# Pooling's projections and four of six gate slabs as seven products of two by two blocks, ahead of HGRN2

## The chip, the cores and the metric

The kernel runs on one core of a Trainium2 chip. The metric is the device time of one launch in microseconds (us); lower is better. Before the change it is 1067.72 us, the median of three runs (1067.62 to 1069.56).

## What is computed

One layer of a hybrid sequence model, on 1024 tokens of 1024 channels, float32. The input is normed and multiplied by one wide matrix `w_in` of 6668 columns. Its columns feed three mixers and their gates. The mixers' results are gated, multiplied by `w_out`, added to the input, and a second gate (`w_pg`) and a last norm follow.

```
u = rms_norm(h, norm_w);  proj = u @ w_in
q, f_logit, i_in, g_hg, u_pool, g_pool, xbc, dt_raw, z = split(proj)
#  768 768   768   768   512     512    1792  12      768  columns
o_hg   = group_rms_norm(hgrn2(q, f_logit, i_in), hg_norm_w) * silu(g_hg)
o_pool = pool_mixer(u_pool) * silu(g_pool)      # windowed means, then a 128x128 matrix per group
y_ssd  = ssd_mixer(xbc, dt_raw) * silu(z)       # state space mixer, normed afterwards
h = h + concat(o_hg, o_pool, o_ssd) @ w_out
out = rms_norm(h + sigmoid(h @ w_pg) * (p @ w_pe))
```

## The kernel before, in words

Float32 products are made of three products of rounded parts (`mm3`, lines 166 to 169): each operand is split into `hi`, rounded, and `lo`, the rest. `u`, transposed, stands as `uh` and `ul` on chip for the whole first half. A weight is loaded into `raw` (two buffers, L135), cast to `hi` on ScalarE (L142) and subtracted to `lo` on VectorE (L143); there are four pairs of `hi` and `lo`. `wsplit` gives these two a priority of 400 steps, and evacuations of a result get 500.

There are two forms of projection. `cm_proj(j)` (L171) leaves 128 channels on the partitions and streams all 1024 tokens in two halves of 512: 48 matmuls of 128x512. `tm_tile` (L184) leaves 128 tokens on the partitions and streams 256 channels of a slab: 24 matmuls of 128x256 for each of eight token tiles.

The order of the program text is: the norm of x with the first slab of V; two more slabs of V (L271), evacuated into `O`, a part of the tile `big` (L233); small values of the state space mixer; six heads of HGRN2 (`hg_proj`, `hg_mix`), which read V from `O` and write their result there; the state space mixer, with 14 channel tiles (`conv_tile`) and four groups (`ssd_group`); three slabs of HGRN2's gate g (L618); pooling, with four times two channel tiles (L641 to 677); three slabs of the gate z (L710); the output projection in two halves of its rows (`ab`) and four slabs each (L742), whose operands overwrite `uh` and `ul` by `fill`; the last gate and norm. A planner places each instruction on its engine, taking ready work by priority (order in the text, moved up by the offsets above) and by estimated times; on the chip each engine then runs its own list in order. SyncE (SP) issues all the loads and stores spoken of here, in order too. Scratch space is handed out by an `Arena` over one tile of 13 x 1024 words, `ar`, the longest free first.

Of the kernel before, what the change touches and what calls it, by code (L numbers as in the profile page):

```python
# [46 lines left out]
class Arena:  # L47
    """Space of one tile, handed out in program order, the longest free first."""
# [29 lines left out]
def body(ctx: ExitStack, tc: tile.TileContext, x, pT, wcm, wtm, wdt, wo, wg, we, nw, fw, cst, prm, out):  # L78
# [9 lines left out]
    a2s = ctx.enter_context(ExitStack())  # L88
    a2p = a2s.enter_context(tc.tile_pool(name="a2p", bufs=1))
# [4 lines left out]
    a2w = 13 * 1024  # L94
    ar = Arena(a2p.tile([P, a2w], F32, name="ar"), a2w)
# [23 lines left out]
    acc = [big[:, 6144 + i * 1024 : 6144 + (i + 1) * 1024].rearrange("p (c t) -> p c t", t=P) for i in range(2)]  # L119
    blk = [cp.tile([P, NT, 32], F32, name=f"blk{i}") for i in range(2)]  # L120
    for a in blk + acc:
        G.memset(a, 0.0)
# [43 lines left out]
    def mm3(o, sh, sl, mh, ml, first, last):  # L166
        T.matmul(out=o, lhsT=sh, rhs=mh, start=first, stop=False)  # L167
        T.matmul(out=o, lhsT=sh, rhs=ml, start=False, stop=False)  # L168
        T.matmul(out=o, lhsT=sl, rhs=mh, start=False, stop=last)  # L169

    def cm_proj(j, evac):  # L171
        """channels of tile j by all tokens: evac(half, psum [P, 512])"""
        cm_want(j)
        hi, lo = pieces.pop(("c", j))
        for half in range(2):
            b = bank("pj")
            c = slice(half * 512, half * 512 + 512)
            for k in range(KD):
                w = slice(k * P, (k + 1) * P)
                mm3(b, hi[:, w], lo[:, w], uh[:, k, c], ul[:, k, c], k == 0, k == KD - 1)  # L180
            with tc.high_priority(offset=EPRIO):
                evac(half, b)
# [15 lines left out]
    def x_norm(t):  # L198
        xt, _ = xs_in[t]
# [4 lines left out]
    def x_turn(t):  # L204
        xt, h = xs_in[t]
        for q in range(2):
# [4 lines left out]
            split_out(b.rearrange("p (k t) -> p k t", t=P), slice(q * 4, q * 4 + 4), slice(t * P, (t + 1) * P))  # L211
        ar.give(h)

    def x_tile(t):
        x_norm(t)
        x_turn(t)

    def split_out(src, ks, cols, scale=None):
        """src -> uh (rounded) and ul (the rest)"""
        hi, lo = uh[:, ks, cols], ul[:, ks, cols]  # L220
        if scale is None:
            A.copy(hi, src)  # L222
            V.tensor_tensor(out=lo, in0=src, in1=hi.bitcast(F32), op=ALU.subtract)  # L223
# [4 lines left out]
    O = big[:, 0:6144].rearrange("p (c n) -> p c n", n=768)  # L228
    dtr = cp.tile([P, NT, NSH], F32, name="dtr")

    def v_evac(s):
        def f(t, b):
            A.copy(O[:, t, s * 256 : s * 256 + 256], b[:, :256])  # L233
# [8 lines left out]
    nc.sync.dma_start(xs_in[1][0], x[P : 2 * P, :])  # L242
    raws.append(wload(tm_src("v", 0)[0][1], 1024))
    for t in range(2, NT):
        nc.sync.dma_start(xs_in[t][0], x[t * P : (t + 1) * P, :])
    with tc.manual_schedule(engines={mybir.EngineType.DVE, mybir.EngineType.Activation, mybir.EngineType.Pool}):
# [22 lines left out]
    ar.give(nwb_h)  # L269
    ar.give(jx_h)  # L270
# [82 lines left out]
    def hg_mix(h):  # L353
# [9 lines left out]
        def scores(b, X, n, cs_):  # L363
            """b[s, c, :] = the keys of s by the queries X of its block of 32"""
# [6 lines left out]
        def place(b, w, nc_, c0, m0, lo, off, cnt, per):  # L371
            """masked columns [off, off + cnt) of each node of b -> columns lo.. of each node of w in the blocks"""
# [7 lines left out]
        def carry(w):  # L380
            """keys and decays from nodes of w to nodes of 2 w"""
# [8 lines left out]
        # within nodes of 4: the queries, decayed over 0, 1, 2 and 3 steps  # L390
# [10 lines left out]
        # queries decayed from their node's start: the first node of four into Q, the rest into XB  # L401
# [11 lines left out]
        # within nodes of 16  # L413
# [44 lines left out]
        # keys with tokens on partitions  # L458
# [10 lines left out]
        for c in range(NT):  # L469
# [37 lines left out]
    def conv_tile(j, nxt):  # L507
        """projection of channel tile j of xbc, convolution and silu: [P, S]"""
# [25 lines left out]
    xw = [big[:, 6144 + i * 768 : 6144 + (i + 1) * 768] for i in range(2)] + [cp.tile([P, 768], F32, name=f"xw{i}") for i in range(2)]  # L534
    nx = [0]

    def ssd_group(g, Bc, Cc):
# [12 lines left out]
        for c in range(NT):  # L550
            tk = slice(c * P, (c + 1) * P)
            r0 = c * NSH + 3 * g
            E = sp.tile([P, 3, P], F32, tag="E", bufs=3, name="E")
# [6 lines left out]
            cbm = sp.tile([P, P], F32, tag="cbm", bufs=2, name="cbm")  # L560
# [27 lines left out]
            if c < NT - 1:  # L588
                cur = sp.tile([P, DG], F32, tag="hst", bufs=2, name="hst")
# [8 lines left out]
    # tiles of xbc: x 0..5, B 6..9, C 10..13  # L598
    plan = ((0, (6, 10, 0, 1)), (1, (7, 11, 2)), (2, (8, 12, 3, 4)), (3, (9, 13, 5)))
    order = [12 + j for _, js in plan for j in js]  # L600
    for g, js in plan:
# [9 lines left out]
        if g == 3:  # L611
            tm_want("g", 0)
# [5 lines left out]
    for s in range(3):  # L618
        tm_want("g", s)
        pcs = [pieces.pop(("g", s, i)) for i in range(2)]  # L620

        def ge(t, b, s=s):
            sg = sp.tile([P, 256], F32, tag="sg", bufs=2, name="sg")
            A.activation(sg, b, AF.Silu)  # L624
            for i in range(2):
                h = 2 * s + i
                V.scalar_tensor_tensor(  # L627
                    out=O[:, t, h * P : (h + 1) * P], in0=O[:, t, h * P : (h + 1) * P], scalar=rsh[:, h, t : t + 1],
                    in1=sg[:, i * P : (i + 1) * P], op0=ALU.mult, op1=ALU.mult)

        for t in range(NT):
            tm_tile("g", s, 256, t, ge, pcs)
            if t == 4:
                if s < 2:
                    want(("g", s + 1, 0), tm_src("g", s + 1)[0][0], 1024)
                else:
                    cm_want(26)

# [1 line left out]
    PO = []  # L640
    for g, win in enumerate(WINS):  # L641
        (U, Uh), (B0, B0h), (B1, B1h) = ar.take(1024), ar.take(1024), ar.take(1024)

        def ue(half, b, U=U):
            A.copy(U[:, half * 512 : half * 512 + 512], b)

        cm_proj(26 + g, ue)
        cm_want(30 + g)
        src, bufs, d, n = U, [B0, B1], 1, 0
        while d < win:  # L650
            dst = bufs[n % 2]
            V.tensor_tensor(out=dst[:, d:], in0=src[:, d:], in1=src[:, : S - d], op=ALU.add)
            V.tensor_copy(dst[:, :d], src[:, :d])
            src, d, n = dst, 2 * d, n + 1
        dst = bufs[n % 2]
        V.tensor_tensor(out=src[:, : win - 1], in0=src[:, : win - 1], in1=cs[:, C_INV : C_INV + win - 1], op=ALU.mult)
        V.tensor_tensor(out=dst[:, : win - 1], in0=src[:, : win - 1], in1=U[:, : win - 1], op=ALU.subtract)
        V.scalar_tensor_tensor(out=dst[:, win - 1 :], in0=src[:, win - 1 :], scalar=1.0 / win, in1=U[:, win - 1 :], op0=ALU.mult, op1=ALU.subtract)
        ar.give(Uh)
        ar.give((B0h, B1h)[(n + 1) % 2])  # L660
        po, poh = ar.take(1024)
        PO.append((po, poh))

        def gpe(half, b, po=po):
            A.activation(po[:, half * 512 : half * 512 + 512], b, AF.Silu)

        cm_proj(30 + g, gpe)
        if g < 3:
            cm_want(26 + g + 1)
        else:  # L670
            tm_want("z", 0)
        for half in range(2):
            c = slice(half * 512, half * 512 + 512)
            b = bank("mx")
            T.matmul(out=b, lhsT=pr[:, P_PW + g * P : P_PW + (g + 1) * P], rhs=dst[:, c], start=True, stop=True)
            V.scalar_tensor_tensor(out=po[:, c], in0=b, scalar=pr[:, P_PS + g : P_PS + g + 1], in1=po[:, c], op0=ALU.mult, op1=ALU.mult)
        ar.give((B0h, B1h)[n % 2])

# [241 lines left out]
```

## Time and profile before

| | |
|---|---|
| median of the runs | 1067.72 us |
| the profiled execution, first to last instruction (its span) | 1066.3 us |
| TensorE matmul (PE) busy | 1044.2 us, 98% |
| VectorE (DVE) busy | 549.0 us, 51% |
| ScalarE (ACT) busy | 400.8 us, 38% |
| GpSimd (POOL) busy | 38.9 us, 4% |
| bytes moved by DMA | 63.83 MB |

No other time is given for the profiled execution than its span; the median of the runs is 1.4 us above it. Matmuls are pipelined: one lasts longer than the distance from it to the next, so the rate is read from start to start. A few per cent of the matmul records can be missing. In the rows, "idle <- X" is time in which an engine sat still, and what it was waiting for.

### The profile page before, as it was taken

The page shows a single profiled execution, that of the slowest core. Times are in us where ns is not written, and L with a number is a line of the kernel's source. Part 1 is how long each engine was busy: PE and PEld are TensorE (multiplying, and loading weights), DVE is VectorE, ACT ScalarE, POOL GpSimd, SP SyncE. Part 2 cuts the span into 40 slices and gives each one's busy share as a digit, 9 for nine tenths or more (in the row PEclk, how much of TensorE's full clock was granted, in tenths as well). Part 3 has the DMA queues.
Part 4 walks back from the last instruction along what each step waited for, and adds up shares of the span by engine and source line. Part 5 has one row for each costly group of instructions (what it writes and reads, how often), then busy time and mean ns, then how long its engine had stood idle before and what let it go on. Part 6 is the DMA issues. An engine that isn't in the chain of part 4 may idle for free.

```text
span 1066.3 us, 19848 instructions
## 1 busy us (share of the span) xinstructions
PE 1044.2 (98%) x8508; PEld 940.4 (88%) x8508; DVE 549.0 (51%) x1090; ACT 400.8 (38%) x842; POOL 38.9 (4%) x69
## 2 busy tenths in 40 slices
PE   8999999999999999999999999999999999999997
PEld 7998778777878788878999777999999999999997
DVE  6413766776674768577832224325532452354444
ACT  6424244323445566656722112126410330143323
POOL 2000000000001000000000000002100000000002
PEclk9999999999999999999999999999999999999999
DMA  7212101010101122122112111111223241111003
GB/s 289 82 41 84 41 21 41 22 41 21 41 21 41 65 75 79 41 79 61 38 44 76 40 40 40 40 41 41 70 87 127 66 139 40 41 41 41 2 19 140
DMA packets 23671, 63.83 MB, mean 60 GB/s; under 512 B 2624, under 2 KB 11168, under 8 KB 23328
## 3 DMA queue, kind: packets, MB, share of 16 engines
q1 hardware_dynamic: 23440, 62.52, 17.6%
q8 instruction: 66, 1.08, 0.4%
q14 instruction: 21, 0.17, 0.1%
q10 hardware_dynamic: 144, 0.07, 0.0%
HBM read 58.33 MB, written 4.24 MB: 59 GB/s over the span
## 4 chain that ended last, share of the span: by engine, by line
PE 85%; DVE 10%; ACT 2%; DMA 1%; POOL 1%; issue 1%; POOLq 0%; ACTq 0%; DVEq 0%
PE b_pj L167 24%; PE b_pj L168 24%; PE b_pj L169 24%; DVE ar L356 5%; PE b_mx L580 1%; PE b_sc L478 1%; PE b_mx L473 1%; PE b_mx L475 1%; DVE lo L143 1%; DVE blk L375 1%; PE b_sc L369 1%; DMA E<-cumd 1%; PE b_mx L688 1%; ACT hi L142 1%; PE b_mx L583 1%; PE b_mx L704 1%
## 5 line engine op out<-in xcount | busy, mean ns | idle before, releaser
L167 PE MATMUL b_pj<-hi,uh 128*128 128x256 f32 (+1 forms) x1344 | 380.2, 283 | 0.2 <-ACT uh L222 0.2
L168 PE MATMUL b_pj<-lo,uh 128*128 128x256 f32 (+1 forms) x1344 | 378.4, 282 | 0.2
L169 PE MATMUL b_pj<-hi,ul 128*128 128x256 f32 (+1 forms) x1344 | 378.1, 281 | 0.2 <-DVE ul L223 0.2
L167 PEld LDWEIGHTS b_pj<-hi,uh 128*128 128x128 f32 x1344 | 253.4, 189 | 1.0 <-ACT uh L222 0.5
L168 PEld LDWEIGHTS b_pj<-lo,uh 128*128 128x128 f32 x1344 | 252.9, 188 | 1.0 <-DVE lo L143 0.6
L169 PEld LDWEIGHTS b_pj<-hi,ul 128*128 128x128 f32 x1344 | 252.8, 188 | 0.5 <-DVE ul L223 0.4
L167 PE MATMUL b_pj<-uh,hi 128*128 128x512 f32 x544 | 220.0, 404 | 0.0
L169 PE MATMUL b_pj<-uh,lo 128*128 128x512 f32 x544 | 219.4, 403 | 0.0
L168 PE MATMUL b_pj<-ul,hi 128*128 128x512 f32 x544 | 218.5, 402 | 0.0
L143 DVE TENSOR_TENSOR lo<-raw,hi 128x1024 fp32r<-128x1024 f32 (+1 forms) x76 | 93.1, 1225 | 145.9 <-ACT hi L142 130.0
L142 ACT CAST hi<-raw 128x1024 fp32r<-128x1024 f32 (+1 forms) x76 | 79.7, 1048 | 206.1 <-PE b_pj L169 106.1
L168 PEld LDWEIGHTS b_pj<-ul,hi 128*128 128x128 f32 x544 | 102.3, 188 | 23.6 <-issue 0.7
L167 PEld LDWEIGHTS b_pj<-uh,hi 128*128 128x128 f32 x544 | 102.3, 188 | 23.2 <-ACT hi L142 0.7
L169 PEld LDWEIGHTS b_pj<-uh,lo 128*128 128x128 f32 x544 | 102.3, 188 | 22.9
L356 DVE TENSOR_TENSOR ar<-ar 128x512 f32<-128x512 f32 (+8 forms) x168 | 94.1, 597 | 6.5 <-PE b_sc L447 4.9
L522 DVE SCALAR_TENSOR_TENSOR ar<-ar,pr 128x1021 f32<-128x1021 f32 (+2 forms) x42 | 53.8, 1280 | 3.4 <-ACT ar L514 2.9
L556 ACT ACTIVATE E<-E,sm 128x128 f32<-128x128 f32 x96 | 32.3, 393 | 24.4 <-DMA E<-cumd 9.2
L766 DVE TENSOR_TENSOR big<-xr,b_pj 128x256 f32<-128x256 f32 x32 | 13.5, 420 | 48.9 <-PE b_pj L169 48.4
L768 DVE TENSOR_TENSOR big<-big,b_pj 128x256 f32<-128x256 f32 x32 | 13.4, 420 | 43.4 <-PE b_pj L169 43.4
L627 DVE SCALAR_TENSOR_TENSOR big<-big,rsh,sg 128x128 f32<-128x128 f32 x48 | 14.7, 349 | 28.8 <-ACT sg L624 28.7
L513 ACT COPY ar<-b_pj 128x512 f32<-128x512 f32 x28 | 16.3, 581 | 33.1 <-PE b_pj L169 33.1
L812 ACT ACTIVATE junk<-sg 128x256 f32<-128x256 f32 x32 | 13.4, 418 | 40.3 <-DVE sg L810 40.3
(184 smaller groups left out, 1066.6 us busy)
## 6 DMA issues: line engine op xcount, KB each, us to landing
raw<-wcm SPq DMA_DIRECT2D x34, 512.0 KB, 3.2
raw<-wtm SPq DMA_DIRECT2D x16, 512.0 KB, 3.3
raw<-wo SPq DMA_DIRECT2D x16, 512.0 KB, 3.4
E<-cumd SPq DMA_DIRECT2D x32, 192.0 KB, 3.0
ar<-x SPq DMA_DIRECT2D x8, 512.0 KB, 9.1
xr<-x SPq DMA_DIRECT2D x32, 128.0 KB, 2.4
raw<-wg SPq DMA_DIRECT2D x8, 512.0 KB, 3.5
out<-big SPq DMA_DIRECT2D x8, 512.0 KB, 2.6
```

The costliest lines, as they stand in the source:

```text
L142: A.copy(hi[:, :width], raw[:, :width])
L143: V.tensor_tensor(out=lo[:, :width], in0=raw[:, :width], in1=hi[:, :width].bitcast(F32), op=ALU.subtract)
L167: T.matmul(out=o, lhsT=sh, rhs=mh, start=first, stop=False)
L168: T.matmul(out=o, lhsT=sh, rhs=ml, start=False, stop=False)
L169: T.matmul(out=o, lhsT=sl, rhs=mh, start=False, stop=last)
L356: mul = lambda o, x, y: V.tensor_tensor(out=o, in0=x, in1=y, op=ALU.mult)
L513: A.copy(xp[:, c], b)
L522: V.scalar_tensor_tensor(out=y[:, d:], in0=xp[:, : S - d], scalar=cw(i), in1=y[:, d:], op0=ALU.mult, op1=ALU.add)
L556: A.activation(E[:, i, :], E[:, i, :], AF.Relu, scale=-1.0, bias=cum[:, r0 + i : r0 + i + 1])
L627: V.scalar_tensor_tensor(out=O[:, t, h * P : (h + 1) * P], in0=O[:, t, h * P : (h + 1) * P], scalar=rsh[:, h, t : t + 1], in1=sg[:, i * P ...
L766: V.tensor_tensor(out=H[:, t, qc], in0=xr, in1=b, op=ALU.add)
L768: V.tensor_tensor(out=H[:, t, qc], in0=H[:, t, qc], in1=b, op=ALU.add)
```

## The change

Strassen's scheme in Winograd's form: a product of two by two blocks in seven products of blocks instead of eight. `u` is cut into four blocks, two halves of the tokens by two halves of its 1024 channels; the weights into two halves of these channels by two tiles (or slabs) of columns. Each of the seven products runs through `mm3`, with half the depth (four steps of 128 instead of eight).

- `build_sums` makes four sums of blocks of `uh + ul` in `big` and splits them into eight tiles `SH`, `SL` of 128 x 2048, in a space of their own (`spool`). This stands after the slabs of V in the text, and may not be placed ahead of the last transposition of x.
- V no longer goes to `O`, since `big` is now the scheme's scratch space (an `Arena` called `bg`); it goes through a small tile to an array `vd` in DRAM and is loaded back into `O` ahead of HGRN2 (24 stores, 6 loads).
- Pooling stands ahead of HGRN2: `st_cm` computes two channel tiles at once, four times (84 matmuls of 128x512 instead of 96). Its gated result goes to `pod` in DRAM (four stores) and comes back at the output projection (four loads).
- `st_tm` computes two slabs at once, twice: z0 with z1, z2 with g0 (336 matmuls of 128x256 instead of 384). The silu of each goes to `gzd` in DRAM (32 stores of 128 KB). z comes back in eight loads in `z_gate`, called beside `y_norm` in the second slab of the output projection; g0 in eight loads beside the slab g1.
- g1 and g2 stay as they were, and the first `fill` moves from the slab z2 to the slab g2.
- `ar` and its pool are opened after the scheme's space is closed. The small tile `sg` has four buffers instead of two, and `xr` shares them.

```diff
+    sst = ctx.enter_context(ExitStack())
+    spool = sst.enter_context(tc.tile_pool(name="spool", bufs=1, reuse_waits="tile"))
+    SH = [spool.tile([P, 4, 512], F32R, name=f"sh{i}") for i in range(4)]
+    SL = [spool.tile([P, 4, 512], F32R, name=f"sl{i}") for i in range(4)]
...
+    def build_sums():
+        for i, j in ((1, 0), (1, 1), (0, 0), (0, 1)):
+            V.tensor_tensor(out=quad(uf, i, j), in0=quad(uh, i, j).bitcast(F32), in1=quad(ul, i, j).bitcast(F32), op=ALU.add)
+        V.tensor_tensor(out=Q22, in0=Q21, in1=Q22, op=ALU.add)
+        V.tensor_tensor(out=Q21, in0=Q11, in1=Q21, op=ALU.subtract)
+        V.tensor_tensor(out=Q11, in0=Q22, in1=Q11, op=ALU.subtract)
+        V.tensor_tensor(out=Q12, in0=Q12, in1=Q11, op=ALU.subtract)
+        for q, hi, lo in zip((Q22, Q11, Q21, Q12), SH, SL):
+            A.copy(hi, q)
+            V.tensor_tensor(out=lo, in0=q, in1=hi.bitcast(F32), op=ALU.subtract)
...
+    def st_cm_w(j0, j1):
+        r0, r1 = wload(wcm[j0], 1024), wload(wcm[j1], 1024)
...
+        w0 = wsplit(r0, 1024)
+        with tc.high_priority(offset=WPRIO):
+            V.tensor_tensor(out=t1, in0=b12, in1=b11, op=ALU.subtract)
+            V.tensor_tensor(out=t3, in0=b22, in1=b12, op=ALU.subtract)
+        w1 = wsplit(T_[:, :1024], 1024)
+        with tc.high_priority(offset=WPRIO):
+            V.tensor_tensor(out=t2, in0=t3, in1=b11, op=ALU.add)
+            V.tensor_tensor(out=t4, in0=b21, in1=t2, op=ALU.subtract)
+        w2 = wsplit(T_[:, 1024:], 1024)
+        w3 = wsplit(b22, 512)
...
+        return {1: part(w0, 0), 2: part(w0, 1), 5: part(w1, 0), 7: part(w1, 1), 6: part(w2, 0), 4: part(w2, 1), 3: part(w3, 0)}
...
+    def st_cm(W, o0, o1):
+        X, Y, Z = bank("mx"), bank("pj"), bank("sc")
...
+        prod(X, 1, True)
+        cp_(o0[:, h0], X)
+        prod(Y, 5, True)
+        cp_(o1[:, h1], Y)
+        prod(X, 6, False)
+        cp_(o1[:, h0], X)
+        prod(Z, 2, True)
+        add_(o0[:, h0], Z)
+        prod(X, 7, False)
+        add_(o1[:, h1], X)
+        prod(Y, 3, False)
+        add_(o1[:, h0], Y)
+        prod(X, 4, False)
+        cp_(o0[:, h1], X)
...
+    def st_tm(s0, s1, fin):
...
+        X = [bank("mx") for _ in range(4)]
+        w4()
+        for o, i in ((c11, 1), (c12, 6), (c22, 7)):
+            for t in prod(X, i, i == 1):
+                with tc.high_priority(offset=EPRIO):
+                    A.copy(o[t], X[t][:, :256])
+            {1: w5, 6: w3, 7: w2}[i]()
+        for t in prod(X, 4, False):
+            fin(4 + t, 0, X[t][:, :256])
+        Y = [bank(("pj", "sc")[t // 2]) for t in range(4)]
+        for o, i in ((c22, 5), (c12, 3)):
+            for t in prod(Y, i, i == 5):
+                with tc.high_priority(offset=EPRIO):
+                    V.tensor_tensor(out=o[t], in0=o[t], in1=Y[t][:, :256], op=ALU.add)
+                fin((4 if i == 5 else 0) + t, 1, o[t])
...
+    W = st_cm_w(26, 27)
+    for g0 in (0, 2):
+        (U0, U0h), (U1, U1h) = bg.take(1024), bg.take(1024)
+        st_cm(W, U0, U1)
+        W = st_cm_w(30 + g0, 31 + g0)
...
+        st_cm(W, G0, G1)
+        if g0 == 0:
+            W = st_cm_w(28, 29)
+        for (g, U, Uh), Gt in zip(pos, (G0, G1)):
+            A.activation(Gt, Gt, AF.Silu)
+            V.tensor_tensor(out=U, in0=U, in1=Gt, op=ALU.mult)
+            nc.sync.dma_start(pod[g], U)
...
+    for i, slabs in enumerate(((5, 6), (7, 2))):
+        def gz_fin(t, n, b, i=i):
+            sg = sp.tile([P, 256], F32, tag="sg", bufs=4, name="sg")
+            with tc.high_priority(offset=EPRIO):
+                A.activation(sg, b, AF.Silu)
+            nc.sync.dma_start(gzd[:, t, (2 * i + n) * 256 : (2 * i + n) * 256 + 256], sg)
...
+    sst.close()
...
+    for h in range(HEADS):
+        nc.sync.dma_start(O[:, :, h * P : (h + 1) * P], vd[:, :, h * P : (h + 1) * P])
...
+    def z_gate(t):
+        sg, sgh = ar.take(768)
+        nc.sync.dma_start(sg, gzd[:, t, :768])
+        V.tensor_tensor(out=Y[:, t, :], in0=Y[:, t, :], in1=sg, op=ALU.mult)
...
                 if ab == 0 and q == 1:
+                    z_gate(t)
                     y_norm(t)
```

In `st_cm` the pooling steps of a pair (windowed sums, then a 128x128 matrix on TensorE) stand between the `st_cm_w` of the pair's gate and the gate's `st_cm`; both are otherwise as before.

## Rows read from the trace of the kernel before

**Rows 1.** The page: span, and TensorE's busy time, share and instructions.
```profile
span 1066.3 us, 19848 instructions
PE 1044.2 (98%) x8508; PEld 940.4 (88%) x8508; DVE 549.0 (51%) x1090; ACT 400.8 (38%) x842; POOL 38.9 (4%) x69
```

**Rows 2.** Stages: from:to, length, busy us (instructions) by engine, clock, DMA share, GB/s.
```profile
33.00:88.00 55.00, 55.00 (x460) 55.00 (x459) 11.06 (x18) 15.12 (x29) 0.00 (x0) 1.00 0.18 60
...
541.00:590.00 49.00, 49.00 (x376) 47.03 (x375) 14.35 (x37) 9.95 (x19) 0.00 (x0) 1.00 0.14 44
590.00:697.00 107.00, 107.00 (x531) 87.60 (x530) 35.94 (x51) 19.60 (x32) 0.00 (x0) 1.00 0.12 40
697.00:763.00 66.00, 64.43 (x548) 63.99 (x547) 33.08 (x75) 34.96 (x102) 10.62 (x16) 1.00 0.17 53
```

**Rows 3.** TensorE's waits: who waited for whom, us in total, times, longest.
```profile
PE b_sc L369 <- DVE ar L356: 6.2, 12, 0.7
PE b_mx L210 <- DVE ar L202: 2.8, 3, 1.6
```

**Rows 4.** Timeline of TensorE, 128x512 matmuls of one projection: start us, us.
```profile
96.61 0.40 PE L167 MATMUL b_pj<-uh,hi 128*128 128x512 f32 x1
...
110.65 0.40 PE L167 MATMUL b_pj<-uh,hi 128*128 128x512 f32 x1
```

**Rows 5.** Timeline of VectorE in a gate slab, one row per token tile.
```profile
540.96 0.62 DVE L627 SCALAR_TENSOR_TENSOR big<-big,rsh,sg 128x128 f32<-128x128 f32 x2 [2.17 <-ACT sg L624]
...
555.21 0.62 DVE L627 SCALAR_TENSOR_TENSOR big<-big,rsh,sg 128x128 f32<-128x128 f32 x2 [2.23 <-ACT sg L624]
```

**Rows 6.** Timeline of VectorE: end of x's transposition, and a later weight split.
```profile
36.28 1.29 DVE L223 TENSOR_TENSOR ul<-b_mx,uh 128x512 fp32r<-128x512 f32 x2 [0.77 <-ACT uh L222]
...
64.24 1.23 DVE L143 TENSOR_TENSOR lo<-raw,hi 128x1024 fp32r<-128x1024 f32 x1 [18.59 <-ACT hi L142]
```

**Rows 7.** VectorE by line and shape: busy us, mean ns, idle us before and releaser.
```profile
L143 DVE TENSOR_TENSOR lo<-raw,hi 128x1024 fp32r<-128x1024 f32 x74 | 90.5, 1223 | 142.1 <-ACT hi L142 126.1 <-PE b_mx L675 13.6 <-DMA xr<-x 2.1
L356 DVE TENSOR_TENSOR ar<-ar 128x512 f32<-128x512 f32 x84 | 57.9, 707 | 5.9 <-PE b_sc L447 4.9
L223 DVE TENSOR_TENSOR ul<-b_mx,uh 128x512 fp32r<-128x512 f32 x32 | 20.5, 685 | 4.6 <-ACT uh L222 4.6
...
L766 DVE TENSOR_TENSOR big<-xr,b_pj 128x256 f32<-128x256 f32 x32 | 13.5, 420 | 48.9 <-PE b_pj L169 48.4 <-DMA xr<-x 0.5
...
L738 DVE TENSOR_SCALAR ar<-ar,rsy 128x192 f32<-128x192 f32 x32 | 8.2, 316 | 13.1 <-POOL rsy L130 13.1
...
L573 DVE TENSOR_TENSOR ar<-ar,pr 128x768 f32<-128x768 f32 x8 | 7.6, 952 | 0.0
```

**Rows 8.** ScalarE by line and shape, columns as in rows 7.
```profile
L142 ACT CAST hi<-raw 128x1024 fp32r<-128x1024 f32 x74 | 77.5, 1047 | 203.9 <-PE b_pj L169 105.0 <-PE b_pj L168 97.2 <-DMA raw<-wtm 1.8
...
L716 ACT ACTIVATE sg<-b_pj 128x256 f32<-128x256 f32 x24 | 9.1, 381 | 34.5 <-PE b_pj L169 34.5
```

**Rows 9.** DMA issues by transfer: count, KB each, median us to landing.
```profile
raw<-wcm SPq DMA_DIRECT2D x34, 512.0 KB, 3.2
...
ar<-x SPq DMA_DIRECT2D x8, 512.0 KB, 9.1
...
out<-big SPq DMA_DIRECT2D x8, 512.0 KB, 2.6
...
cumd<-rows SPq DMA_DIRECT2D x1, 48.0 KB, 1.5
```

**Rows 10.** SyncE's waits ahead of its DMA issues, columns as in rows 3.
```profile
SPq L135 <- DVE lo L143: 427.8, 48, 21.0
```

**Rows 11.** Timeline of TensorE: first matmul of HGRN2's projections, first that reads V.
```profile
87.94 0.39 PE L167 MATMUL b_pj<-uh,hi 128*128 128x512 f32 x1
...
137.23 0.39 PE L473 MATMUL b_mx<-big 128*128 128x128 f32 x2
```

More of the change, by code (lines that the diff above doesn't have):

```diff
@@ L164, in tm_want, with mm3 @@
             want((kind, s, i), srcs[i], 4 * n)
[L166 to L169, printed above, removed]
+    def mm3(o, sh, sl, mh, ml, first, last, more=False):
+        T.matmul(out=o, lhsT=sh, rhs=mh, start=first, stop=False, skip_group_check=more)
+        T.matmul(out=o, lhsT=sh, rhs=ml, start=False, stop=False, skip_group_check=more)
+        T.matmul(out=o, lhsT=sl, rhs=mh, start=False, stop=last, skip_group_check=more)
     def cm_proj(j, evac):
@@ L232, in f @@
         def f(t, b):
[L233 removed]
+            vs = sp.tile([P, 256], F32, tag="sg", bufs=4, name="vs")
+            A.copy(vs, b[:, :256])
+            nc.sync.dma_start(vd[:, t, s * 256 : s * 256 + 256], vs)
             if s == 2:
@@ L275, in body @@
             tm_tile("v", s, (256, 256, 268)[s], t, v_evac(s), pcs)
+    with tc.issue_after(turned.ins):
+        build_sums()
+    bg.give(ufh)
+    def st_cm_w(j0, j1):
+        r0, r1 = wload(wcm[j0], 1024), wload(wcm[j1], 1024)
+        b11, b21, b12, b22 = r0[:, :512], r0[:, 512:1024], r1[:, :512], r1[:, 512:1024]
+        T_, Th = bg.take(2048)
+        t1, t3, t2, t4 = (T_[:, i * 512 : i * 512 + 512] for i in range(4))
+        w0 = wsplit(r0, 1024)
[8 more added lines that the diff above has]
+        w3 = wsplit(b22, 512)
+        bg.give(Th)
+        part = lambda w, i: tuple(z[:, i * 512 : i * 512 + 512] for z in w)
+        return {1: part(w0, 0), 2: part(w0, 1), 5: part(w1, 0), 7: part(w1, 1), 6: part(w2, 0), 4: part(w2, 1), 3: part(w3, 0)}
@@ new lines, in st_cm, with prod, cp_, add_ @@
+    def st_cm(W, o0, o1):
+        X, Y, Z = bank("mx"), bank("pj"), bank("sc")
+        h0, h1 = slice(0, 512), slice(512, 1024)
+        def prod(b, i, first):
+            (wh, wl), (ah, al) = W[i], AOP[i]
+            for k in range(4):
+                w = slice(k * P, (k + 1) * P)
+                mm3(b, wh[:, w], wl[:, w], ah[:, k, :], al[:, k, :], first and k == 0, k == 3, not first)
+        def cp_(o, b):
+            with tc.high_priority(offset=EPRIO):
+                A.copy(o, b)
+        def add_(o, b):
+            with tc.high_priority(offset=EPRIO):
+                V.tensor_tensor(out=o, in0=o, in1=b, op=ALU.add)
+        prod(X, 1, True)
[12 more added lines that the diff above has]
+        cp_(o0[:, h1], X)
@@ L333, in body @@
+    a2w = 13 * 1024
+    ar = Arena(a2p.tile([P, a2w], F32, name="ar"), a2w)
+    O = big[:, 0:6144].rearrange("p (c n) -> p c n", n=768)
+    acc = [big[:, 6144 + i * 1024 : 6144 + (i + 1) * 1024].rearrange("p (c t) -> p c t", t=P) for i in range(2)]
+    for a in acc:
+        G.memset(a, 0.0)
+    for h in range(HEADS):
+        nc.sync.dma_start(O[:, :, h * P : (h + 1) * P], vd[:, :, h * P : (h + 1) * P])
     ssh = cp.tile([P, HEADS, NT], F32, name="ssh")
@@ L615, in body @@
             ar.give(yh)
[L618 to L637, printed above, removed]
@@ L640, in body @@
[L640 to L677, printed above, removed]
```

190 lines of the change are left out of this document (145 added, 45 removed).

## The prediction, on record before the changed kernel ran

> **What bounds the kernel now.** I read the page first. TensorE is busy for 1044.2 of the span's 1066.3 us, VectorE for half of it [rows 1]. Such a busy time counts overlapping matmuls, so I looked next at stages. The ones that the change shortens are full: TensorE is busy through the whole of 541 to 590 us (gate g) and 590 to 697 us (pooling), while VectorE has 14 of 49 and 36 of 107 us and ScalarE less; only around 697 to 763 us, where the norm of the state space mixer runs, are 1.6 us missing [rows 2]. The list of waits agrees: TensorE's longest entry is 6.2 us inside HGRN2, the next 2.8 us in the first transpositions [rows 3], and neither lies in a stage that the change shortens. So in these stages the end is set by the number of matmuls and their rate, and a matmul less is its whole distance to the next less. That distance, start to start: 60 steps between the two rows of a channel tile take 14.04 us, 0.234 us for 128x512 [rows 4]. In a gate slab five token tiles of 24 matmuls take 14.25 us, 2.85 us a tile or 0.1188 us for 128x256, what lies between tiles included [rows 5].
>
> **What the change removes.** Four pairs of channel tiles go from 96 to 84 matmuls each: 48 x 0.234 = 11.2 us. Two pairs of slabs go from 384 to 336: 96 x 0.1188 = 11.4 us. The transpositions, the pooling matrices and all else on TensorE stay in number. Sum: 22.6 us.
>
> The Trainium skill has another rate: "TensorE: Matmul & The Clock Gate", section "Back-to-back issue gap", gives 131 ns as the sustained spacing for 512 columns in a stream of weight loads and matmuls, and about 216 ns for a single gap. By the first the channel tiles would give 48 x 0.131 = 6.3 us instead of 11.2 and the time would be 4.9 us later than mine. The trace has 0.234 us over 60 steps in just such a stream, so I give that rate 1 chance in 100, within the first case below.
>
> **The sums of u.** Twelve VectorE operations of 128x2048 and four casts. No such shape is in the trace. From the row of 128x1024 (1.22 us) it is 2.45 us if time goes with width, from that of 128x512 (0.71 us) 2.83 us, and 1.22 us if width cost nothing [rows 7]; the cast is 2.1 us by the 1.05 us row [rows 8]. I take 2.45: 29.4 us of VectorE and 8.4 of ScalarE. The cover is the two slabs of V. The last part of x is turned at 37.6 us [rows 6] and the first channel tile starts at 87.9 us [rows 11]; in 33 to 88 us VectorE has 11 of 55 us and ScalarE 15 [rows 2]. So 50 us stand against 29 + at most 11. Cost 0; without the cover it would be up to 34 us. What is late next is the small chain of step sizes after the slabs, which TensorE would notice by at most one such operation, 2.8 us.
>
> **Weights.** A pair of channel tiles costs VectorE 3.5 splits of 1.22 us, four sums of 0.71 and three additions from PSUM of 0.69 (the 128x512 row with a PSUM source): 9.2 us, four times 36.7. Pooling brings 14 steps of 1.22 and four products with the gate, 22 us [rows 7]. Together 59 us beside 336 x 0.234 = 78.6 us of TensorE. A pair of slabs costs VectorE 11 x 1.22 + 12 x 0.42 = 18.5 us, ScalarE 7 x 1.05 + 28 x 0.38 = 18 us [rows 7, 8], beside 39.9 us. Neither engine becomes the bound by its sum; order can still hurt. One set of weights fills all four hi/lo pairs. They come free after the fourth, fifth, sixth and seventh product (a product is 12 x 0.234 = 2.8 us), so the next set's first pair has 8.4 us for a cast and a subtraction of 2.3 us, the second and third as much, since they are wanted one and two products later. That leaves 6 us for waiting behind other work, whose longest single operation is 1.3 us. In the slabs a product is 5.7 us and the margin wider. In `st_cm` a bank is emptied beside another product of 2.8 us; the copy or addition takes 0.7.
>
> At such hand-overs the kernel now loses little: 12 waits behind VectorE in HGRN2 are 0.5 us each [rows 3]. I count seven new ones (four channel pairs, two slab pairs, back to HGRN2) and take 3 us in all; the bounds are 0 and the 48 us of the slow case below.
>
> **Parking.** Each 128x256 store leaves from one of four small tiles. The stores shown take 1.5 us (48 KB) and 2.6 us (512 KB) [rows 9]; with the silu's 0.38 us a tile is back after at most 3.0 us, and it is wanted again after four results of 12 x 0.1188 = 1.43 us, 5.7 us. V's results come about every 2.85 us. Cost 0, bound 1 us a slab. SP issues these stores in its one list; behind a store that waits stand weight loads. They have room: today they wait 427.8 us in total for a buffer's split [rows 10], and the split at 64 us serves a matmul at 88 us [rows 6, 11].
>
> V's reload is six loads of 512 KB, between 3.2 and 9.1 us each [rows 9], so 19 to 55 us. The first head reads V 49.3 us after its projections begin [rows 11], and each later head reads a slice of its own, a head later: hidden at both ends. What queues behind them are weights: four channel tiles (45 us) can be split before, so 0 to 10 us; I take 0. The scratch that HGRN2's first evacuation needs is free when the last-but-one product ends, 5.7 us before TensorE gets there.
>
> **The end.** z's product and the norm move into one slab of the output projection. There a token tile costs VectorE 0.42 + 0.95 + 4 x 0.316 = 2.63 us [rows 7] of 2.85; with two splits, 23.5 of 22.8 us. It spills 0.7 us into the next slab; the evacuation that TensorE needs has the priority. Between -1.6 us (today's idle there [rows 2]) and +2; I take 0.
>
> **Sum.** 1066.3 - 22.6 + 3 = 1046.7 us of span; the median of the runs stands 1.4 us above the profiled span, so 1048.1 us.
>
> **The rivals.**
> - *VectorE's order holds up the weights.* For: in the second gate pair, 9 pooling steps (11 us) stand beside the splits; and by the order in which `bg` hands out space, the first weights of the slabs land where pooling's windows of group 2 and 3 were, so a load of 3.2 us, two sums, a cast and a split (8 us in all) can start only after them. Against: splits have 400 steps of priority. Price: 11 less the margin of 6, and the 8: 13 us on top of no loss (1045.1): 1058, say 1053 to 1064.
> - *The buffers are handed over too late (slower).* If a set's pairs are not given in the order in which they come free, each of the seven hand-overs costs a whole chain on TensorE: load 3.2, two sums 1.4, cast 1.05, split 1.22, 6.9 us, 48 us in all: 1067.7 - 22.6 + 48 = 1093. It makes the kernel slower from 3.2 us a hand-over. For: one set takes all four pairs and both raw buffers. Against: the margin above, and that buffers are given by estimated times.
> - *The reload of V delays weights.* 10 us at HGRN2's start: 1055.
> - *The products don't get cheaper*: matmuls on the new tiles `SH` run slower by the eighth saved. Nothing in the trace speaks for it, as all operands have the same type and shape: 1067.
> - *No loss at all, and today's idle at the norm goes too*: 1043.5.
>
> **How the numbers follow.** Forecast 0.60 (its own range 1045 to 1053); VectorE's order 0.22; V's reload 0.05; no loss and a gain 0.04; no cheaper products 0.02; buffers too late 0.07. To hold 8 in 10 the range reaches from 1044 to 1061, into the second case. A measurement of this kernel can tell 0.2%, 2.1 us. Faster: the first four, less 0.02 for the tail of VectorE's order: 0.89. Same: no cheaper products and half that tail, 0.03. Slower: buffers too late and the other half, 0.08.
>
> **What would show it.** 48 matmuls of the 512 form and 96 of the 256 form less, at unchanged distances; the stretch of the scheme, from the end of V to HGRN2's first matmul, at 78.6 + 79.8 us and pooling's matrices, with TensorE full; no wait of TensorE behind L143's counterpart over 1 us; HGRN2, the state space mixer and everything from the output projection on as long as now. A wait of some 5 us or more at the start of a pair means one of the two rivals on weights: behind pooling's steps it is the first, behind a load or a cast with VectorE free the second. I am wrong if TensorE's idle grows by more than 8 us, or if the distances in the new products differ from 0.234 and 0.119.

## The result and the profile after

The changed kernel takes 1053.62 us (median of four runs, 1052.85 to 1054.85) against 1067.88 (four runs): a ratio of 0.9867, 95% interval 0.9853 to 0.9881, 14.3 us faster. 1048.1 was forecast, with 1044 to 1061 as the range. The profiled run is the slowest of the four; its span is 1053.0 us, 13.3 below that of before.

The page of the kernel after, its span and TensorE; it answers to [rows 1]:

```profile
span 1053.0 us, 19902 instructions
PE 1027.2 (98%) x8364; PEld 923.7 (88%) x8364; DVE 620.3 (59%) x1156; ACT 447.9 (43%) x904; POOL 39.9 (4%) x69
```

There are 144 matmuls less, 48 + 96, as the prediction counted them. VectorE is busy 71 us longer and is off the path for nearly all of it.

The stages of the kernel after (columns as in [rows 2]): V, pooling by the scheme, four slabs by the scheme, and, after HGRN2, the state space mixer and the gate slab g1, the gate slab g2:

```profile
33.00:87.70 54.70, 54.70 (x457) 54.70 (x457) 39.03 (x34) 22.04 (x32) 0.00 (x0) 1.00 0.29 96
87.70:174.90 87.20, 86.53 (x360) 66.04 (x359) 62.22 (x98) 34.57 (x50) 0.00 (x0) 1.00 0.20 69
174.90:258.40 83.50, 81.52 (x674) 80.81 (x673) 34.10 (x45) 36.25 (x74) 1.92 (x2) 0.98 0.37 118
...
703.70:735.00 31.30, 28.34 (x233) 27.86 (x232) 26.76 (x69) 24.69 (x85) 11.27 (x16) 0.95 0.40 120
```

Two stages stand out at a glance: the slabs by the scheme lack 2.0 us of TensorE and show a clock of 0.98, the slab g2 lacks 3.0 us and shows 0.95. To set them against before, both traces are cut at the first matmul of each stage, in us:

| stage | before | after |
|---|---|---|
| start to the end of V | 87.94 | 87.73 |
| six gate slabs, pooling: before, three pieces (first slab of g; g1, g2, pooling, z0, z1; last slab) | 36.12 + 187.23 + 27.24 = 250.59 | – |
| the same after (scheme; g1; last slab g2) | – | 170.64 + 35.59 + 31.29 = 237.52 |
| HGRN2 and the state space mixer | 410.52 | 409.73 |
| output projection, slabs 0 and 1 / 2 to 7 | 48.22 / 148.25 | 48.07 / 148.69 |
| the rest | 120.75 | 121.30 |

The whole gain, 13.1 us of 13.3, lies in the second and third rows; all else moved by 0.8 us or less. Of the 22.6 us forecast there, 9.5 are missing in this execution (by the medians of the runs, 14.3 of 22.6, it is 8.3). 4.1 of them are in the slabs by the scheme (83.46 us; with the scratch handed out in another order, below, the same matmuls take 79.32) and 4.05 in the last slab (31.29 against 27.24).

TensorE's waits in the kernel after (who waited for whom, us in total, times, longest); they answer to [rows 3]:

```profile
PE b_sc L595 <- DVE ar L582: 6.2, 12, 0.7
PE b_mx L806 <- DVE E L788: 2.5, 3, 1.0
PE b_mx L852 <- DVE ul L220: 2.3, 1, 2.3
...
PE b_pj L165 <- ACT hi L139: 1.1, 1, 1.1
PE b_pj L166 <- DVE lo L140: 0.9, 2, 0.5
PE b_mx L479 <- DVE sm L475: 0.7, 1, 0.7
...
PE b_mx L165 <- ACT big L420: 0.3, 1, 0.3
```

The first line is HGRN2's old one. The second (0.7 of it, in g2), third, fourth, fifth and last lead to the two losses.

**The first loss: scratch that a store still reads.** ScalarE in the timeline of the kernel after, where pooling gives way to the first pair of slabs (start us, us; in brackets the idle time before and its releaser):

```profile
180.79 1.04 ACT L139 CAST hi<-big 128x1024 fp32r<-128x1024 f32 x1 [3.02 <-PE b_mx L167]
185.43 1.20 ACT L420 COPY big<-b_mx 128x256 f32<-128x256 f32 x4 [3.60 <-DMA pod<-big]
```

SyncE there:

```profile
177.34 0.33 SPq L529 DMA_DIRECT2D pod<-big  x1
...
179.61 0.33 SPq L529 DMA_DIRECT2D pod<-big  x1
```

The copies of product 1 into their scratch `c11` wait for a store, `pod<-big`: `c11` was given the place of one of pooling's results, whose 512 KB were still on their way out. TensorE at the same time:

```profile
180.47 0.28 PE L167 MATMUL b_mx<-hi,ul 128*128 128x256 f32 x1
...
181.88 0.50 PE L165 MATMUL b_pj<-hi,sh 128*128 128x256 f32 x2 [1.13 <-ACT hi L139]
183.14 0.39 PE L166 MATMUL b_pj<-lo,sh 128*128 128x256 f32 x1 [0.52 <-DVE lo L140]
185.85 0.58 PE L165 MATMUL b_mx<-hi,sh 128*128 128x256 f32 x1 [0.32 <-ACT big L420]
```

The last matmul of product 1 starts at 180.47. The next in TensorE's list is a piece of product 5 (`b_pj<-hi,sh`), which waits for its cast and split; that cast had itself waited for a matmul of product 1 (the bracket at 180.79). Product 6 (`b_mx` again) stands behind the copies. So of the idle pieces that the timeline names, 1.13, 0.52 and 0.32 us, only the last stands at the copies directly; the run give_order below shows that all three go with them. The clock column of the windows, the third from the right, shows what came on top:

```profile
180.00:182.00 2.00, 0.87 (x8) 0.66 (x7) 0.14 (x1) 1.04 (x1) 0.00 (x0) 1.00 0.93 256
...
184.00:186.00 2.00, 1.68 (x9) 1.39 (x8) 0.00 (x0) 0.57 (x3) 0.00 (x0) 0.52 0.08 33
186.00:188.00 2.00, 2.00 (x12) 2.00 (x13) 0.00 (x0) 0.63 (x3) 0.00 (x0) 0.62 0.00 0
```

After the thin stretch that begins at 180 us TensorE ran at 1.2 instead of 2.4 GHz for most of 184 to 188 us: 2 x (0.48 + 0.38) = 1.7 us lost to the clock, beside 2.0 us of idle time that the timeline names.

**The second loss: the norm was pulled forward.** VectorE in the kernel after, in the slab g2, just ahead of the last `fill` steps into `uh` and `ul`:

```profile
726.97 1.00 DVE L926 TENSOR_SCALAR ar<-ar,rsy 128x192 f32<-128x192 f32 x4
727.90 0.61 DVE L890 SCALAR_TENSOR_TENSOR big<-big,rsh,sg 128x128 f32<-128x128 f32 x2
728.43 0.95 DVE L883 TENSOR_TENSOR ar<-ar 128x768 f32<-128x768 f32 x1
729.30 2.06 DVE L220 SCALAR_TENSOR_TENSOR ul<-b_mx,pr,uh 128x512 fp32r<-128x512 f32 x3
```

L883 is z's product and L926 the norm. The text has them in the second slab of the output projection, but the planner placed them as soon as they were ready, in g2, between gating (L890) and the subtraction of `fill` (L220), which TensorE's next transpositions need. Those waited 2.25 us, where the kernel before waited 1.57 us at the same place, in its z2:

```profile
PE b_mx L688 <- DVE ul L226: 1.6, 1, 1.6
```

And again the clock fell, here too as the windows show it:

```profile
730.00:732.00 2.00, 1.90 (x9) 1.90 (x10) 1.36 (x3) 1.87 (x9) 1.06 (x2) 0.55 0.10 34
732.00:734.00 2.00, 2.00 (x12) 2.00 (x12) 1.83 (x7) 2.00 (x8) 0.14 (x1) 0.59 0.00 0
```

That is 2 x (0.45 + 0.41) = 1.7 us. The pulled-forward work costs a second, smaller wait at the start of g2, where the last matmuls of the state space mixer now run: a product that they need (L788) stands behind one of z's products on VectorE.

```profile
704.56 0.95 DVE L883 TENSOR_TENSOR ar<-ar 128x768 f32<-128x768 f32 x1
705.43 0.55 DVE L788 TENSOR_TENSOR E<-E,cbm 128x384 f32<-128x384 f32 x1
...
706.12 0.57 PE L806 MATMUL b_mx<-xw,E 128*64 128x64 f32 x12 [0.71 <-DVE E L788]
```

So of the last slab's 4.05 us, 0.7 are the fill beyond its wait of before, 0.7 this wait, 1.7 clock, and some 0.8 the 14 matmuls of the mixer, which before ended inside the first gate slab (in norm_later below the slab, without a wait, takes 26.48 us; before it took 27.24 with a wait of 1.57).

### The profile page after: what moved, and what is told of

It reads as the page before. It is cut to its first block, busy times and chain, and to the rows that moved or that the text cites. A ratio compares the mean times of both kernels' runs of the same rounds, so it can differ in the third digit from the quotient of the medians.

```text
span 1053.0 us, 19902 instructions
## 1 busy us (share of the span) xinstructions
PE 1027.2 (98%) x8364; PEld 923.7 (88%) x8364; DVE 620.3 (59%) x1156; ACT 447.9 (43%) x904; POOL 39.9 (4%) x69
## 4 chain that ended last, share of the span: by engine, by line
PE 81%; DVE 11%; ACT 3%; DMA 3%; issue 1%; POOL 0%; SPq 0%; POOLq 0%; ACTq 0%; DVEq 0%
PE b_pj L166 19%; PE b_pj L165 19%; PE b_pj L167 19%; DVE ar L582 5%; PE b_mx L165 3%; PE b_mx L167 3%; PE b_mx L166 3%; PE b_mx L806 1%; DVE lo L140 1%; PE b_sc L704 1%; PE b_mx L699 1%; PE b_mx L701 1%; DVE blk L601 1%; PE b_sc L167 1%; PE b_sc L166 1%; PE b_sc L165 1%
## 5 line engine op out<-in xcount | busy, mean ns | idle before, releaser
L165 PE MATMUL b_pj<-hi,uh 128*128 128x256 f32 (+1 forms) x1088 | 309.9, 285 | 0.4 <-ACT uh L216 0.4
L166 PE MATMUL b_pj<-lo,uh 128*128 128x256 f32 (+1 forms) x1088 | 307.3, 282 | 0.4 <-DVE lo L140 0.4
L167 PE MATMUL b_pj<-hi,ul 128*128 128x256 f32 (+1 forms) x1088 | 306.6, 282 | 0.2 <-DVE ul L217 0.2
L166 PEld LDWEIGHTS b_pj<-lo,uh 128*128 128x128 f32 x1088 | 205.8, 189 | 1.1 <-DVE lo L140 0.9
L165 PEld LDWEIGHTS b_pj<-hi,uh 128*128 128x128 f32 x1088 | 205.7, 189 | 0.8 <-ACT uh L216 0.6
L167 PEld LDWEIGHTS b_pj<-hi,ul 128*128 128x128 f32 x1088 | 205.5, 189 | 0.4 <-DVE ul L217 0.4
L166 PE MATMUL b_pj<-ul,hi 128*128 128x512 f32 x416 | 168.8, 406 | 0.0
L165 PE MATMUL b_pj<-uh,hi 128*128 128x512 f32 x416 | 168.3, 404 | 0.0
L167 PE MATMUL b_pj<-uh,lo 128*128 128x512 f32 x416 | 167.8, 403 | 0.0
L139 ACT CAST hi<-raw 128x1024 fp32r<-128x1024 f32 (+1 forms) x72 | 73.9, 1026 | 175.6 <-PE b_pj L167 99.0
L140 DVE TENSOR_TENSOR lo<-raw,hi 128x1024 fp32r<-128x1024 f32 (+1 forms) x72 | 85.9, 1194 | 103.5 <-ACT hi L139 91.7
L166 PEld LDWEIGHTS b_pj<-ul,hi 128*128 128x128 f32 x416 | 78.2, 188 | 17.7
L140 DVE TENSOR_TENSOR lo<-big,hi 128x1024 fp32r<-128x1024 f32 x18 | 21.9, 1222 | 14.0 <-ACT hi L139 14.0
```

What stands on the lines that cost most here:

```text
L139: A.copy(hi[:, :width], raw[:, :width])
L140: V.tensor_tensor(out=lo[:, :width], in0=raw[:, :width], in1=hi[:, :width].bitcast(F32), op=ALU.subtract)
L165: T.matmul(out=o, lhsT=sh, rhs=mh, start=first, stop=False, skip_group_check=more)
L166: T.matmul(out=o, lhsT=sh, rhs=ml, start=False, stop=False, skip_group_check=more)
L167: T.matmul(out=o, lhsT=sl, rhs=mh, start=False, stop=last, skip_group_check=more)
```

## The experiments

Times are medians beside the kernel before on the same chip (1068.43 us for the first four, 1068.03 for the last three, nine runs each). The changed kernel's 1053.62 stands beside 1067.88, so a difference from it of some 0.5 us says nothing.

### give_order: hand out the stored places last

```diff
             nc.sync.dma_start(pod[g], U)
-            bg.give(Uh)
         bg.give(G0h)
         bg.give(G1h)
+        for _, _, Uh in pos:
+            bg.give(Uh)
```

The places of the gates, which no store reads, are now the longest free and go out first.

> One edit to the changed kernel: at the end of a pooling pair the gates' scratch is given back ahead of pooling's own, so that in the first slab pair the results of products 1 and 6 lie where the gates were, which no store to DRAM reads. Theory A (the result of product 1 waited for the landing of pooling's store out of the same scratch; TensorE then stood still and ran at the lower clock for some us after): the waits of TensorE at 180 to 186 us and the stretch at half clock go, the slabs' stage is some 4 us shorter, 1049.6 us (1048.5 to 1051). Rival B (weights for product 6 were late anyway, cast and split behind the last pooling pair): a wait of the same size behind L139 or L140 stays, 1053 us. Rival C (parking or relocation costs as a whole, not at one place): no change, 1053.6 us.

Measured: 1049.49 us (1048.60 to 1050.04), ratio 0.9825 (0.981 to 0.984), 4.1 below the changed kernel. Its windows over the scheme's slabs and g2:

```profile
175.80:255.10 79.30, 79.30 (x673) 79.28 (x672) 34.03 (x45) 36.38 (x74) 1.91 (x2) 1.00 0.38 124
...
699.20:728.70 29.50, 26.80 (x233) 26.32 (x232) 24.76 (x65) 23.15 (x81) 10.29 (x14) 1.00 0.43 126
```

ScalarE's first copy of product 1 no longer waits for a store:

```profile
180.56 0.93 ACT L420 COPY big<-b_mx 128x256 f32<-128x256 f32 x3 [1.92 <-DVE big L528]
```

In the slabs TensorE is full, the clock whole, and 83.46 us became 79.32; product 6 now follows product 1 without a gap. An edit that adds no instruction gave back the first loss; its cause is shown. The last window still lacks 2.7 us, at a clock of 1.00: its longest wait is now 2.5 us, longer than that of the kernel after, yet the clock stayed up and the slab took 29.47 instead of 31.29 us, about the 1.7 us that the clock column had.

### norm_later: hold z's product and norm back to where the text has them

```diff
-                if ab == 0 and q == 1:
-                    z_gate(t)
-                    y_norm(t)
+                if ab == 0 and q == 1:
+                    with tc.issue_after(filled.ins):
+                        z_gate(t)
+                        y_norm(t)
```

`filled` is the last subtraction of the fill in the slab before; the lines that hand it out are left out here.

> One edit to the changed kernel: z's product and the state space norm may not be placed on VectorE ahead of the last fill of the first half (in the first slab of the output projection). Theory A (the planner pulled them ahead into the slab g2, beside the tail of the state space mixer and the first fills; a fill's subtraction came 2.25 us late and TensorE ran at half clock for 3.4 us after): the wait at 728 us and the half clock behind it go, 3 us less, 1050.6 us (1049.5 to 1052). Rival B (the fill is late because of the gates of slab g2 itself): the wait stays, 1053.6. Rival C (the work, held back, ends late for the fills of the state space half): a new wait ahead of the second half of the output projection, 1054 or more.

Measured: 1054.26 us (1054.05 to 1055.08), ratio 0.9872 (0.9855 to 0.9888): nothing gained. The last slab came down from 31.29 to 26.48 us, full, but the first two slabs of the output projection went from 48.07 to 53.35. In this run the slabs by the scheme are as in the changed kernel, and the first loss is there, with idle pieces of 1.13, 0.54 and 0.57 us, but the clock stays whole:

```profile
184.00:186.00 2.00, 1.43 (x12) 1.22 (x11) 0.00 (x0) 0.95 (x4) 0.00 (x0) 1.00 0.02 6
```

They take 82.39 us. So the stored places cost 3.1 us by themselves (82.39 against 79.32), and the lower clock, which need not follow, is the rest.

### both: the two edits together

> Both edits. Theory A: the two losses are at different places and add, 1046.6 us (1045.5 to 1048), within 2 us of the sum that leaves out all losses (1045.3). If they don't add, something later takes up the time gained: 1048 to 1050.

Measured: 1050.38 us (1049.86 to 1051.21), ratio 0.9835 (0.982 to 0.9849), not better than give_order alone. The new line among its waits:

```profile
PE b_pj L165 <- DVE big L957: 4.1, 4, 1.2
```

And VectorE's timeline at one of these four:

```profile
765.43 0.78 DVE L929 TENSOR_SCALAR ar<-ar,rsy 128x192 f32<-128x192 f32 x3 [3.09 <-POOL rsy L127]
766.12 0.41 DVE L957 TENSOR_TENSOR big<-xr,b_pj 128x256 f32<-128x256 f32 x1
```

VectorE, in the order that the planner gave it, stands 3.09 us before the scaling (L929) and waits for GpSimd's root of the norm; the evacuation (L957) that TensorE needs is queued behind it. The sum of VectorE's work in that slab, on which the prediction argued, fits; what does not is a chain over three engines within one token tile. Rival C of norm_later (held back, the work makes new waits, 1054 or more) had the time right and the place wrong: the waits are behind evacuations in the first two slabs, not ahead of the second half. The two edits together miss their sum, 1046.6 us, by 3.8 us: here too the first two slabs take 53.36 us.

### norm_spread: two slabs for the norm, and the scaling a tile later

On top of give_order; only the call is shown. `y_scale` is the last part of `y_norm`, `he_ins` the evacuations of the output projection.

```diff
-                if ab == 0 and q == 1:
-                    z_gate(t)
-                    y_norm(t)
+                if ab == 0 and q in (1, 2):
+                    with tc.issue_after(he_ins[-1].ins):
+                        i = (q - 1) * 4 + t // 2
+                        if t % 2 == 0:
+                            z_gate(i)
+                            y_norm(i)
+                        else:
+                            y_scale(i)
```

> The kernel with the scratch given back in the other order, and z's product and the norm spread over two slabs of the output projection: for every second token tile one product with its squares, and its scaling one tile later, each held behind that tile's evacuation. Theory A (the late norm costs the wait of a fill in slab g2, 2.5 us, when it is pulled ahead, and evacuations 4 to 5 us when it is packed into one slab): last slab of g 26.5 us instead of 29.5, the first two slabs of the output projection 48.1 instead of 53.4, 1046.5 us (1045.5 to 1048). Rival: the first fills wait for the gates of g2 themselves or evacuations still stand behind the norm: 1049 to 1051, as with either order before.

Measured: 1046.38 us (median of five runs, 1045.44 to 1046.97), ratio 0.9796 (0.9783 to 0.981). It is the best version, 7.2 us below the changed kernel. VectorE's timeline in the first of the two slabs shows the chain opened up: between product and scaling of a tile now stands an evacuation, and the idle time before the scaling is 1.4 us.

```profile
754.00 0.95 DVE L884 TENSOR_TENSOR ar<-ar 128x768 f32<-128x768 f32 x1
756.52 0.42 DVE L959 TENSOR_TENSOR big<-xr,b_pj 128x256 f32<-128x256 f32 x1 [1.57 <-PE b_pj L167]
758.32 1.01 DVE L931 TENSOR_SCALAR ar<-ar,rsy 128x192 f32<-128x192 f32 x4 [1.38 <-POOL rsy L127]
```

In the second of them VectorE stands 3.09 us before scalings again, three times, but TensorE does not wait there at all (the slab takes 22.67 us, as in the kernel after). Its one wait comes at the start of the slab behind, where the evacuation is queued after a weight split (L140):

```profile
798.08 1.23 DVE L140 TENSOR_TENSOR lo<-raw,hi 128x1024 fp32r<-128x1024 f32 x1 [1.52 <-ACT hi L139]
799.22 0.41 DVE L959 TENSOR_TENSOR big<-xr,b_pj 128x256 f32<-128x256 f32 x1
...
799.69 0.39 PE L165 MATMUL b_pj<-hi,uh 128*128 128x256 f32 x1 [0.57 <-DVE big L959]
```

So the standing still costs TensorE nothing by itself; in the run of both edits it did, with such a chain in every token tile. Which of the two, the spreading or the later scaling, did more was not tried apart. Its stages: scheme 166.48, g1 35.75, g2 26.48: 228.71 against 250.59 before, 21.9 us less.

### placed_plain: the place and the parking, without the scheme

`st_cm` becomes two plain channel tiles (`cm_proj`) copied to the same places, `st_tm` two plain slabs, the sums of u are gone; order, parking and reload stay.

```diff
-    with tc.issue_after(turned.ins):
-        build_sums()
...
-        st_cm(W, U0, U1)
...
+        plain(26 + g0, U0)
...
+        plain(27 + g0, U1)
...
-        st_tm(*slabs, gz_fin)
+        for n, sl in enumerate(slabs):
...
+            for t in range(NT):
+                tm_tile("w", sl, 256, t, lambda t, b, n=n: gz_fin(t, n, b), pcs)
```

> The changed kernel's order and parking without the scheme: no sums of u, pooling's eight tiles and the four slabs by the plain projections (eight products' worth), at the same places, with the same stores and loads. Theory A (place and parking are nearly free but for the late norm; the wait at the slabs belongs to the scheme's scratch): 1053.6 + 22.4 - 4 = 1072 us (1070 to 1073), 4 us over the kernel before at most. Rival C (place and parking lose most of the missing 9 us): 1075 or more. Rival D (the seven products are dearer than seven eighths, place and parking free): 1068.

Measured: 1071.38 us (1070.43 to 1073.15, six runs), ratio 1.003 (1.0018 to 1.0042): the move and the parking cost 3 us by themselves. Its windows over pooling and the four slabs:

```profile
87.80:185.80 98.00, 97.88 (x409) 75.62 (x408) 37.95 (x64) 31.66 (x55) 0.95 (x1) 1.00 0.21 73
185.80:276.70 90.90, 90.90 (x770) 90.90 (x769) 9.96 (x9) 21.49 (x41) 0.95 (x1) 1.00 0.41 127
```

TensorE is full in both, so storing the slabs' gates in pieces of 128 KB costs it nothing. Cut at the first matmuls the two are 97.94 and 90.91, and against them the scheme, undisturbed, saves 10.7 us in pooling (87.2) and 11.6 in the slabs (79.32). The last slab takes 29.35 here too, 2.1 more than before: the norm pulled forward belongs to the move, not to the scheme.

### slabs_plain and pooling_plain: one half of the scheme at a time

On top of give_order, with only the second, or only the first, of placed_plain's replacements.

> The kernel with the scratch given back in the other order, but with the four slabs by the plain projection at the same place (pooling by the scheme, sums of u made). Theory A (each part saves its matmuls times their distance, nothing else): 1049.5 + 96 x 0.1188 = 1060.9 us (1059.5 to 1062). Rival D (the seven products lose to hand-overs in the slabs, where seven weights are made for four): 1057 or less.

> The same, but with pooling's eight channel tiles by the plain projection and the slabs by the scheme. Theory A: 1049.5 + 48 x 0.234 = 1060.7 us (1059.5 to 1062). Rival D for the channel tiles: 1057 or less. Both parts together should give back what the run without the scheme gave, 1071.4.

Measured: slabs_plain 1064.32 us (1063.81 to 1064.73), ratio 0.9966 (0.9952 to 0.9979), 3.4 above what was expected; pooling_plain 1058.54 (1057.68 to 1060.21), ratio 0.9914 (0.99 to 0.9927), 2.2 below. Set against placed_plain, the channel tiles by the scheme give 7.1 us and the slabs 12.8, set against give_order 9.1 and 14.8; neither pair adds up to the 21.9 us between placed_plain and give_order (0.4 us of the difference lies between the chips, by the kernel before). Neither run came out in its expected range: each version has waits of its own. In slabs_plain the plain slabs took 93.01 us instead of 90.91. Its waits of TensorE in that stretch, and ScalarE's timeline there:

```profile
PE b_pj L165 <- ACT sg L541: 1.7, 2, 1.0
```

```profile
186.63 1.28 ACT L541 ACT_TABLE_LOAD   x1
187.92 0.66 ACT L541 ACTIVATE sg<-b_pj 128x256 f32<-128x256 f32 x2
188.47 0.70 ACT L788 ACTIVATE E<-E,sm 128x128 f32<-128x128 f32 x2
189.18 1.28 ACT L789 ACT_TABLE_LOAD   x1
190.47 0.53 ACT L789 ACTIVATE E<-E 128x384 f32<-128x384 f32 x1
```

The planner had put the state space mixer's exponentials (L789, with the step L788 ahead of them) between the slabs' silus (L541), and each change between silu and exponential loads a table, 1.28 us; L788 needs no load. The Trainium skill, "ScalarE: Activation LUTs", section "What ACT_TABLE_LOAD costs", gives 1283 ns for the load, which the rows confirm, and some 1.38 us of drain beside it; here the load at 189.18 starts as the activation before it ends (188.47 + 0.70), and the next follows 1.29 us later, so no drain shows. Half clock also came back in g2, which took 31.09 us in slabs_plain and 30.67 in pooling_plain against 29.47 in give_order.

## Why the prediction came out as it did

The sign and the place were right, and so was the mechanism of the saving; the cost of the hand-overs was sized too small and put on the wrong resources, and the end was priced at nothing. The 1053.62 us lie 0.6 us beyond the forecast's own range (1045 to 1053). They lie inside the whole range, 1044 to 1061, because this had been widened for a rival, VectorE holding up the weights, that is not what happened.

- **Matmuls saved, 22.6 us: right.** The scheme undisturbed saves 10.7 + 11.6 = 22.3. The distances did not change; twelve steps of the 512 form and 36 of the 256 form, inside the scheme's products, in TensorE's timeline of the kernel after:

```profile
98.60 0.39 PE L166 MATMUL b_mx<-ul,hi 128*128 128x512 f32 x1
...
101.39 0.39 PE L166 MATMUL b_mx<-ul,hi 128*128 128x512 f32 x1
...
175.74 0.28 PE L166 MATMUL b_mx<-lo,uh 128*128 128x256 f32 x1
...
180.00 0.28 PE L166 MATMUL b_mx<-lo,uh 128*128 128x256 f32 x1
```

  2.79 / 12 = 0.2325 us and 4.26 / 36 = 0.1183, against 0.234 and 0.1188 in [rows 4, 5]. By an estimate from the 131 ns that the Trainium skill has for 512 columns ("TensorE: Matmul & The Clock Gate", section "Back-to-back issue gap") the channel tiles would have saved 6.3 us; the runs have 10.7, so the row decided rightly.
- **Sums of u, 0: right.** V ends at 87.73 us, before it was 87.94 [rows 11], with VectorE busy 39 of 54.7 us instead of 11 of 55 [rows 2].
- **Weights and hand-overs, 3 us: too small, and this is the step that failed.** Weights were never late by more than 1.1 us, and in give_order, with the same weights, not at all. What was late was scratch: the prediction went through the weights' buffers and through HGRN2's first evacuation, but not through what reads the places on which `c11`, `c12` and `c22` land. A 512 KB store was reading one. It cost 4.1 us (give_order), about 1 to 1.7 of it through the lower clock (norm_later, the windows). The two rivals on weights had the right kind of place, the change from pooling to slabs; the first even argued from the order in which `bg` hands out space, but for the weights, and with readers on VectorE.
- **Parking, 0: right for the silus** (TensorE full over the slabs in placed_plain) and wrong for `pod`, whose stores are the ones that the scratch waited for.
- **V's reload, 0: no sign of a loss.** In the window of the reload TensorE is full while the queues move 314 GB/s:

```profile
262.50:275.00 12.50, 12.50 (x55) 10.04 (x55) 2.45 (x2) 8.42 (x15) 0.00 (x0) 1.00 1.09 314
```

  HGRN2 with the mixer is 0.8 us shorter than before; 1.1 us of that is the small chain of step sizes, which moved ahead into pooling's stage, with a new wait of 0.7 us (L479). The prediction had allowed it up to 2.8 us and priced it at 0.
- **The end, 0: wrong by 2 us, and by 4 with the clock.** The prediction put z's product and norm where the text has them and added up VectorE's busy time there. It left out the 13.1 us for which VectorE had stood before these scalings, waiting for GpSimd, already in the kernel before; its own row of L738 shows them [rows 7]. And the 1.6 us that it took for idle time at the norm were the wait of the fill in z2, the one that grew. The planner moved them ahead, and where they were held (norm_later) the same sum of work still cost TensorE 5.3 us (53.35 against 48.07), through the wait for GpSimd inside each tile (4.1 us of TensorE's waits are named in the run of both edits). norm_spread shows that it can be had for 1.6 us (slabs 2 to 7: 149.87 instead of 148.25) and nothing in the last slab.
- **No wait behind a weight's split of over 1 us, and no idle grown by more than 8 us:** both held. Behind the split (L140) the longest wait was 0.5 us, behind the cast (L139) 1.1; TensorE's idle grew by 3.7 us, from 22.1 to 25.8. So neither of these signs showed the losses; the length of the stretch did. The 9.5 us were some 4.1 us of idle time (2.0 at the scratch, 0.7 more than before at the fill, 0.7 at L806, 0.7 at L479), 3.4 of clock and 1.4 of matmuls that changed their stage (1.1 of the step sizes, 0.8 of the mixer, less the 0.5 by which g1 is shorter); some 0.6 are not traced, most of them in the scheme's slabs. The slabs were to take 79.8 us, took 83.46, and take 79.32 once nothing holds them up.

Over the stages of the table the sum now reads 22.3 (saved) - 4.1 (scratch) - 4.05 (last slab) - 1.1 (matmuls of the step sizes, moved in from HGRN2's stage) = 13.05, of the 13.07 that the table shows; the new wait of 0.7 us and g1, shorter by 0.5, nearly cancel.

What stays open: why an idle stretch is followed by the lower clock in one execution and not in another. 2.5 us left the clock alone in give_order and 2.25 us lowered it in the kernel after. The kernel alone does not decide it: the four executions of the kernel after had mean clocks of 0.994 (1054.85 us, the one profiled) to 0.997 (1052.85 us). Open is also why HGRN2 with the state space mixer takes between 407.9 us (pooling_plain) and 409.9 us (slabs_plain) in versions that have the same text there.

## What to carry to other kernels

When scratch space changes its owner, list what still reads the old content, DMAs to memory included, and hand out first what no store reads: the edit of give_order was worth 4.1 us. Work that is only moved in the text goes where the planner's priorities put it; find the place in the trace, and hold or spread it so that no engine that TensorE waits for has to stand in a chain over other engines in every tile. And a wait can cost more than its length: here 2.25 us of idle time were followed by a loss of 1.7 us through the clock.

## What was not expected of the hardware

An idle stretch of TensorE of 2.25 us (the kernel after), 2.6 (slabs_plain) or 2.5 (pooling_plain) ahead of the last fill was followed by some 3.4 us at 1.2 GHz; 2.5 us in give_order and 2.3 in placed_plain were not, nor 1.57 in the kernel before. The idle pieces at the stored places, 2.0 us in all, were followed by the lower clock in the kernel after; 2.2 us at the same place in norm_later were not. The clock column puts the price at 1.7 us each time (2 x (0.50 + 0.35) in slabs_plain, at 740 to 744 us).
